# Channel-major output stages with streamed weights, and late attention spread beside them, in a hybrid encoder layer on one Trainium2 core

## The chip, the cores and the metric

One core of a Trainium2 chip runs the whole program. The metric is the device time of one execution in microseconds (us). Engines: PE = TensorE (matmul; PEld its weight loads), DVE = VectorE, ACT = ScalarE, POOL = GpSimd, SP = SyncE, which here only issues DMAs.

## The reference, cut to what matters

The sequence has 2048 tokens of 1024 channels, all in float32.

```
h    = rmsnorm(x)
proj = h @ W_in                       # 1024 -> 4096: 4 conv parts, q, k, v, az (512 each)
y_c  = c_b * causal_dwconv(c_c * c_h)            # conv group, 3 taps
z    = q @ k^T / 8                               # 8 heads of 64, strictly causal
a    = exp(log_sigmoid(z) + sum of log_sigmoid(-z) over the keys between key and query)
y_a  = a @ v
y    = group_rmsnorm([y_c, y_a]) * silu([c_z, a_z])
x    = x + y @ W_out                             # 1024 -> 1024
x    = x + sigmoid(rmsnorm(x) @ W_pg + b_pg) * (p @ W_pe)
out  = rmsnorm(x) * final_g
```

## The kernel before, in words

**Numbers and tiles.** Each float32 operand of a large product is a pair of float32r tiles, high (`hh`, `wh`) and low (`hl`, `wl`); a product is three matmuls, high by high, low by high and high by low (L208 to L210 for W_in, L543 to L545 for W_out, W_pg and W_pe). ACT writes the high part as a copy (`wh`, L200), POOL subtracts to get the low part (`wl`, L201). Tokens come in four chunks of 512 with time reversed: chunks 3 and 2 are the early half, chunks 1 and 0 the late half. A step of a projection is three matmuls on 512 columns; a projection tile (128 output channels) has 8 of them for a chunk.

**Projections.** W_in has 32 tiles of 128 channels, each run over the two chunks of a half and streamed twice, half a tile (128x512) at a time, by `load_w` and `split_half` (L187 to L202). Their results are channel-major and are evacuated by DVE.

**Attention.** For 128 queries (a row, j) and 512 keys (kc), `unit_a` (L394 to L422) issues two matmuls for z (L401, L402), two sigmoids on ACT (`s`, L405, and `b`, L407), a scan on DVE (`T`, L415; on the diagonal also L413), a copy of the last column on POOL (`carry`, L419) and the product b·T on DVE (L420). Four rows are a unit. `unit_b` (L424 to L465) then takes four key blocks: four transposes of b (L443), the high part on ACT (`ah`, L447), the low part on DVE (`al`, L448), and the two matmuls into av (L433 with `ah`, L434 with `al`). The av matmuls of a key block come directly after the transposes of the next one:

```
ah = att.tile([P, CH], F32R, tag="ah", bufs=3, ...)          # L445
...
nc.scalar.copy(ah[:, 0:w], tp[:, 0:w])                       # L447
nc.vector.tensor_tensor(out=al[:, 0:w], in0=tp[:, 0:w],
                        in1=ah[:, 0:w].bitcast(F32), op=ALU.subtract)
yield
if late:
    finish()                                                 # the av matmuls of the block before
    yield
late = (ah, al, kb, w)
```

There are 80 units: 24 in the early half (16 of them on the diagonal and so about half as large) and 56 in the late half (16 on the diagonal), head by head.

**Order of the work.** A generator, `attention`, yields after each piece; `run(rate)` pulls `rate` pieces for each projection step: `RATE_E` 0.5 in the early half, `RATE_L` 1.3 in the late half, `RATE_O` 2.0 beside the first blocks of the output stage. So the order of instructions on each engine is fixed when the program is built; the engines wait for each other by semaphores only.

**Output stages.** After the late projections W_out is loaded whole, split (`split_w`, L519 to L539; the low parts half by DVE and half by POOL) and kept on chip. `out_block` (L571) treats 16 blocks of 128 tokens, token-major (`out_prep` scales y by the group norm), and writes x1 to DRAM. W_pg and W_pe are loaded and kept likewise. The last stage (L727 to L780) reads x1 again for each block, transposes it (L742), and computes the gate, the embedding term (`pe`), the sum and the final norm; the last block is treated in quarters.

Of the kernel before, what the change touches and what calls it, by code (L numbers as in the profile page):

```python
# [9 lines left out]
BF16 = mybir.dt.bfloat16  # L10
# [5 lines left out]
P = 128  # L16
# [7 lines left out]
RATE_E = 0.5  # L24
RATE_L = 1.3
RATE_O = 2.0
LAG = 1
WARM = 9


def build(tc, xt_d, xr_d, pt_d, win_d, wout_d, wpg_d, wpe_d, cst_d, bpg_d, fg_d, out_d):
    """All token axes run backwards in time, so that attention scans forwards over keys."""
    nc = tc.nc
    ctx = ExitStack()
    with ctx:
# [7 lines left out]
        yg_d = dram.tile([SEQ // P, P, KT, P], F32, name="yg_d")  # L43
        x1_d = dram.tile([SEQ, DM], F32, name="x1_d")
        kE_d = dram.tile([NH, P, 2, CH], F32, name="kE_d")
        vE_d = dram.tile([NH, P, 2, CH], F32, name="vE_d")

# [1 line left out]
        cst = const.tile([P, 40], F32, name="cst")  # L49
# [3 lines left out]
        c_b = cst[:, 36:40]  # L53
        # first: column 0 clear, then the identity, so that row q holds a one at column q + 1
# [20 lines left out]
        rs1 = const.tile([P, 16], F32, name="rs1")  # L75
        rr = const.tile([P, 32], F32, name="rr")
# [9 lines left out]
        attx = ExitStack()  # L86
        att = attx.enter_context(tc.tile_pool(name="att", bufs=1, side="right"))
        NS = 2
# [7 lines left out]
        projx = ExitStack()  # L96
        pj = projx.enter_context(tc.tile_pool(name="pj", bufs=1, side="left"))
# [3 lines left out]
        hT, rx, rB = {}, {}, {}  # L101

        def load_x(c, kt, name, tag="w1", bufs=4):
            xt = (pj if tag == "w1" else att).tile([P, CH], F32, tag=tag, bufs=bufs, name=f"{name}{c}_{kt}")
            nc.sync.dma_start(xt, xt_d[c, kt])
            return xt

        def load_x_first(c, between=None):
            tiles = []
            for i, tag in enumerate(("q1", "q1", "q2", "q2") if c == 3 else ("kk", "kk")):  # L110
                t = att.tile([P, 2, CH], F32, tag=tag, bufs=2, name=f"xf{c}_{i}")
                for f in range(2):
                    nc.sync.dma_start(t[:, f], xt_d[c, 2 * i + f])
                    tiles.append(t[:, f])
                if i == 1 and between:
                    between()
            if c == 2:
                for i, tag in enumerate(("ke2", "ke3", "ve2", "ve3")):
                    tiles.append(load_x(c, 4 + i, "xf", tag, 1))
            return tiles  # L120

        def x_split(c, kt, xt):
            hh = pj.tile([P, CH], F32R, tag=f"hh{kt}", bufs=2, name=f"hh{c}_{kt}")
            hl = pj.tile([P, CH], F32R, tag=f"hl{kt}", bufs=2, name=f"hl{c}_{kt}")
            nc.scalar.activation(hh, xt, AF.Copy, scale=g_norm[:, kt:kt + 1])  # L125
            nc.vector.scalar_tensor_tensor(out=hl, in0=xt, scalar=g_norm[:, kt:kt + 1],  # L126
                                           in1=hh.bitcast(F32), op0=ALU.mult, op1=ALU.subtract)
            hT[c, kt] = (hh, hl)

        def norm_first(c, xts, tag):  # L130
            """r of a chunk whose x is on chip."""
            acc = None
            for kt in range(KT):
                sq = att.tile([P, CH], F32, tag="bt", bufs=10, name=f"xsq{c}_{kt}")
                if kt in (3, 5, 7):
                    nc.gpsimd.tensor_tensor(out=sq, in0=xts[kt], in1=xts[kt], op=ALU.mult)
                else:
                    nc.scalar.activation(sq, xts[kt], AF.Square)
                if kt == 0:
                    acc = sq  # L140
                else:
                    nc.vector.tensor_tensor(out=acc, in0=acc, in1=sq, op=ALU.add)
            ssp = bank(tag, 1, f"ssp{c}")
            token_sums(ssp, acc)
            norm_r(c, ssp)

        def norm_later(c):
            """r of a chunk, beside other work: a step for each tile of x."""
            acc = att.tile([P, CH], F32, tag="ke2", bufs=1, name=f"acc{c}")
            for kt in range(KT):  # L150
                xt = load_x(c, kt, "xt")
                sq = xt if kt else acc
                nc.scalar.activation(sq, xt, AF.Square)
                if kt:
                    nc.vector.tensor_tensor(out=acc, in0=acc, in1=sq, op=ALU.add)
                yield
            ssp = bank("aux", 1, f"ssp{c}")
            token_sums(ssp, acc)
            norm_r(c, ssp)

        def token_sums(ssp, sq):
            for b in range(4):
                nc.tensor.matmul(ssp[:, 2 * b:2 * b + 2], sq[:, b * P:(b + 1) * P], ones2,
                                 start=True, stop=True)

        def norm_r(c, ssp):
            r, r2 = rr[:, 8 * c:8 * c + 4], rr[:, 8 * c + 4:8 * c + 8]
            nc.vector.tensor_scalar(out=r, in0=ssp[:, 0:8:2], scalar1=1.0 / DM, scalar2=EPS,
                                    op0=ALU.mult, op1=ALU.add)
            nc.gpsimd.tensor_tensor(out=r, in0=r, in1=nhalf[:, 0:4], op=ALU.pow)  # L170
            nc.vector.scalar_tensor_tensor(out=r2, in0=r, scalar=1.0 / HD, in1=r, op0=ALU.mult,
                                           op1=ALU.mult)
            rx[c] = (r, r2)

        def norm_spread(c, tag="aux"):
            r, _ = rx[c]
            rT = bank(tag, 2 if tag == "tr" else 1, f"rT{c}")
            for b in range(4):
                nc.tensor.transpose(rT[:, b * P:(b + 1) * P], r[:, b:b + 1].to_broadcast([P, P]), ident)
            rB[c] = pj.tile([P, CH], F32, tag="rB", bufs=2, name=f"rB{c}")  # L180
            nc.scalar.copy(rB[c], rT)

# [1 line left out]
        wq, wt = [], {}  # L184

        def load_w(f):
            """Fetch and split half f of the next tile in line."""  # L187
            if not wq:
                return
            t, tag = wq[0]  # L190
            split_half(t, f, tag, pj, "wh", "wl")
            if f == 1:
                wq.pop(0)

        def split_half(t, f, tag, pool, th, tl):
            raw = pj.tile([P, CH], F32, tag="wr", bufs=2, name=f"wr{tag}_{t}_{f}")
            nc.sync.dma_start(raw, win_d[t, f])
            wh = pool.tile([P, CH], F32R, tag=th, bufs=3, name=f"wh{tag}_{t}_{f}")
# [640 lines left out]
```

## Time and profile before

| | before |
|---|---|
| time, median of 3 runs | 1733.89 us (1732.41 to 1736.25) |
| span of the profiled execution | 1731.2 us |
| busy: PE, DVE, ACT, POOL | 93%, 69%, 45%, 32% of the span |
| DMA | 152.46 MB, mean 88 GB/s |

How to read it: a span is the time from the first to the last recorded instruction of the profiled execution; the profile gives no other time of its own for that execution, and the median of the runs is 2.7 us above it. Busy times of PE overlap, since matmuls are pipelined: a 512-column matmul is shown with 0.39 to 0.50 us, while the next one starts 0.23 us after it. So 93% is not 93% of PE's peak. By place, the program is start (0 to 50 us), early half (to 525), late half with most of attention (to 1270), output stage (to 1488) and gate stage (to the end); the last av matmul of attention starts at 1311.09 us.

### The profile page before, as it was taken

To read this page: it belongs to the slowest core of one execution; us is meant where nothing else is said; L and a number is where in the kernel's file an instruction comes from. 1 tells how busy PE (TensorE), PEld (TensorE's weight loads), DVE (VectorE), ACT (ScalarE), POOL (GpSimd) and SP (SyncE) were. 2 spreads that over 40 slices of the span, in tenths; PEclk is the share of its full clock that TensorE was granted. 3 is DMA by queue.
4 is the path that set the end of the run, shared out by engine and by line. 5 is a ranking of instruction groups with operands and counts; after the bars stand their busy time and mean duration, and the time that the engine had idled before them with its cause. 6 is when DMAs were issued, how large, how long until landed. Compare 5 with 4: busy or idle time off the path is not lost.

```text
span 1731.2 us, 22033 instructions
## 1 busy us (share of the span) xinstructions
PE 1609.0 (93%) x7726; PEld 1287.3 (74%) x7726; DVE 1187.5 (69%) x1691; ACT 771.7 (45%) x1516; POOL 550.7 (32%) x607
## 2 busy tenths in 40 slices
PE   7899999999998899889898999899979999999998
PEld 5787777777877677767776777677757778788887
DVE  7676666666566898996889699978995533233333
ACT  5345345345345555564556455645563422122222
POOL 5322432432453422224223332233552111122221
PEclk9999999999999999999999999999999999999999
DMA  5413513513414311221112311221144743222221
GB/s 188 129 43 104 146 50 98 147 55 98 128 56 118 77 37 50 66 69 49 43 43 71 76 48 38 73 62 49 31 152 145 246 150 133 77 82 83 83 79 49
DMA packets 84207, 152.46 MB, mean 88 GB/s; under 512 B 9472, under 2 KB 27904, under 8 KB 84096
## 3 DMA queue, kind: packets, MB, share of 16 engines
q1 hardware_dynamic: 62304, 125.10, 24.7%
q10 hardware_dynamic: 21792, 25.96, 4.3%
q8 instruction: 61, 1.00, 0.2%
q14 instruction: 50, 0.41, 0.1%
HBM read 92.30 MB, written 33.55 MB: 73 GB/s over the span
## 4 chain that ended last, share of the span: by engine, by line
PE 55%; DVE 25%; issue 8%; ACT 5%; POOL 3%; DMA 2%; SPq 0%; ACTq 0%; DVEq 0%; POOLq 0%
DVE T L415 10%; PE pp L208 8%; PE pp L210 8%; PE pp L209 7%; DVE b L420 5%; DVE al L448 4%; PE tp L443 3%; PE pg L545 3%; PE pg L543 3%; PE pg L544 3%; PE po L543 3%; PE po L544 3%; PE po L545 3%; PE av L434 2%; ACT s L405 2%
## 5 line engine op out<-in xcount | busy, mean ns | idle before, releaser
L208 PE MATMUL pp<-hh,wh 128*128 128x512 f32 x1024 | 427.9, 418 | 0.1
L209 PE MATMUL pp<-hl,wh 128*128 128x512 f32 x1024 | 407.6, 398 | 4.4 <-DVE hl L126 4.4
L210 PE MATMUL pp<-hh,wl 128*128 128x512 f32 x1024 | 408.7, 399 | 0.0
L415 DVE TENSOR_TENSOR_SCAN T<-s,carry,small 128x513 f32<-128x513 f32 x192 | 269.7, 1411 | 28.8 <-ACT s L405 28.2
L405 ACT ACTIVATE s<-z 128x512 f32<-128x512 f32 (+1 forms) x320 | 172.2, 538 | 181.2 <-PE z L402 129.4
L201 POOL TENSOR_TENSOR wl<-wr,wh 128x512 fp32r<-128x512 f32 x128 | 184.5, 1442 | 210.4 <-ACT wh L200 152.4
L447 ACT CAST ah<-tp 128x512 fp32r<-128x512 f32 (+1 forms) x320 | 164.3, 525 | 183.1 <-PE tp L443 151.3
L420 DVE TENSOR_TENSOR b<-b,T 128x512 f32<-128x512 f32 (+1 forms) x320 | 228.0, 717 | 18.9
L210 PEld LDWEIGHTS pp<-hh,wl 128*128 128x128 f32 x1024 | 195.0, 190 | 42.3
L209 PEld LDWEIGHTS pp<-hl,wh 128*128 128x128 f32 x1024 | 196.4, 192 | 37.1 <-DVE hl L126 7.6
L448 DVE TENSOR_TENSOR al<-tp,ah 128x512 fp32r<-128x512 f32 (+1 forms) x320 | 188.3, 602 | 50.6 <-ACT ah L447 49.6
L208 PEld LDWEIGHTS pp<-hh,wh 128*128 128x128 f32 x1024 | 195.4, 191 | 29.4 <-ACT hh L125 0.7
L419 POOL COPY carry<-T 128x1 f32<-128x1 f32 x192 | 64.5, 336 | 366.7 <-DVE T L415 331.5
L443 PE MATMUL tp<-first,b 128*128 128x128 f32 x1088 | 176.6, 277 | 2.1 <-DVE b L420 1.3
L407 ACT ACTIVATE b<-z 128x512 f32<-128x512 f32 (+1 forms) x320 | 170.4, 532 | 0.0
L443 PEld LDWEIGHTS tp<-first,b 128*128 128x128 f32 x1088 | 139.1, 143 | 40.6 <-DVE b L420 5.8
L200 ACT CAST wh<-wr 128x512 fp32r<-128x512 f32 x128 | 79.4, 621 | 95.0 <-PE pp L209 73.1
L434 PE MATMUL av<-al,vv 128*128 128x512 f32 x192 | 71.9, 377 | 41.9 <-DVE al L448 41.6
L543 PE MATMUL po<-woh,yh 128*128 128x512 f32 x256 | 102.7, 402 | 2.5 <-ACT yh L567 2.5
L544 PE MATMUL po<-wol,yh 128*128 128x512 f32 x256 | 102.1, 400 | 2.2 <-DVE wol L531 2.2
L543 PE MATMUL pg<-wgh,xh 128*128 128x512 f32 (+1 forms) x272 | 102.5, 377 | 1.4 <-ACT xh L744 1.4
L545 PE MATMUL pg<-wgh,xl 128*128 128x512 f32 (+1 forms) x272 | 102.7, 378 | 0.0
(149 smaller groups left out, 2551.6 us busy)
## 6 DMA issues: line engine op xcount, KB each, us to landing
wr<-in_win_dram SPq DMA_DIRECT2D x128, 256.0 KB, 2.7
q<-sh SPq DMA_DIRECT2D x64, 128.0 KB, 2.4
q<-sl SPq DMA_DIRECT2D x64, 128.0 KB, 2.3
yg_d<-gg ACTq DMA_DIRECT2D x32, 256.0 KB, 2.3
yt<-yg_d SPq DMA_DIRECT2D x16, 512.0 KB, 3.3
xb<-in_xr_dram SPq DMA_DIRECT2D x16, 512.0 KB, 3.8
x_d<-x ACTq DMA_DIRECT2D x16, 512.0 KB, 2.6
z<-x_d SPq DMA_DIRECT2D x16, 512.0 KB, 3.3
```

The lines of the kernel that those rows point to most:

```text
L201: nc.gpsimd.tensor_tensor(out=wl, in0=raw, in1=wh.bitcast(F32), op=ALU.subtract)
L208: nc.tensor.matmul(pp, wh[:, sl], hh, start=(kt == 0), stop=False)
L209: nc.tensor.matmul(pp, wh[:, sl], hl, start=False, stop=False)
L210: nc.tensor.matmul(pp, wl[:, sl], hh, start=False, stop=(kt == KT - 1))
L405: nc.scalar.activation(s[:, 1:n + 1], zp[:, 0:n], AF.Sigmoid, scale=-0.125)
L415: nc.vector.tensor_tensor_scan(T[:, m:n + 1], s[:, m:n + 1], zeros.to_broadcast([P, n + 1 - m]), T[:, m - 1:m] if diag else carry[:, j:j + ...
L420: nc.vector.tensor_tensor(out=bt[:, 0:n], in0=bt[:, 0:n], in1=T[:, 0:n], op=ALU.mult)
L443: nc.tensor.transpose(tp[:, j * P:(j + 1) * P], bt[:, kb * P - k0:(kb + 1) * P - k0], ident)
L448: nc.vector.tensor_tensor(out=al[:, 0:w], in0=tp[:, 0:w], in1=ah[:, 0:w].bitcast(F32), op=ALU.subtract)
L543: nc.tensor.matmul(pp, ah, wh[:, sl], start=first, stop=False)
L544: nc.tensor.matmul(pp, ah, wl[:, sl], start=False, stop=False)
L545: nc.tensor.matmul(pp, al, wh[:, sl], start=False, stop=last)
```

## The change

All stages become channel-major. W_out and W_pg are appended to W_in as 16 further tiles (numbers 32 to 39 and 40 to 47) and streamed and split again for each of the four chunks, as W_in is; nothing stays resident. That doubles the weight halves split (`wh` on ACT, `wl` on POOL) from 128 to 256. The tail order is out(3), gate(3), out(2), gate(2), out(1), gate(1), out(0), gate(0).

- Late attention is ordered by chunk: all heads of chunk 1, then all heads of chunk 0. Its rows are spread over the late projections (131 rows in the order of PE), out(3) (17), gate(3) (23), out(2) (16), gate(2) (23) and out(1) (14); the early half has 96. The rates are 0.72 (early) and 0.92 (late projections and these stages).
- K, Q and V of a unit always go through DRAM (`fetch_units`, two units ahead), so SP issues 987 DMAs where it issued 520.
- z and the sigmoids of a row are issued one row earlier (`row_z` before `row_scan`; three `s` and three `T` buffers). In `second`, `al` is issued one key block after `ah`, and the av matmuls two key blocks after the transposes (four buffers of `ah` and `al`).
- b·T of odd rows goes from DVE to POOL: 160 of 320 (96 of 512 columns, 32 of 384, 32 of 128).
- The group norm and gate of y (`y_prep`, one tile of 128 channels at a time) run beside the gate stage before; the residual's square sum and the final norm work on channel-major tiles, with sums on POOL. The 128 transposes of x1 fall away. `final(c)` runs beside the next output stage; `final(0)` stands alone at the end.
- Small steps (conv taps, stores, transposes of v, norms) are put off by some steps by `later` and `tick`.

```
-RATE_E = 0.5
-RATE_L = 1.3
-RATE_O = 2.0
...
+RATE_E, RATE_L = 0.72, 0.92
...
+            eng = nc.gpsimd if j % 2 else nc.vector
+            eng.tensor_tensor(out=bt[:, 0:w], in0=bt[:, 0:w], in1=T[:, 0:w], op=ALU.mult)
...
+            for i in range(6):
+                if i < 4:
...
+                    nc.scalar.copy(ah[:, 0:nj * P], tp[:, 0:nj * P])
+                if 1 <= i <= 4:
+                    tp, ah, al, _, w = st[i - 1]
+                    nc.vector.tensor_tensor(out=al[:, 0:w], in0=tp[:, 0:w], in1=ah[:, 0:w].bitcast(F32),
+                                            op=ALU.subtract)
                 yield
...
+                if i >= 2:
+                    _, ah, al, kb, w = st.pop(i - 2)
+                    nc.tensor.matmul(av[:, 0:w], v[:, kb], ah[:, 0:w], start=diag and kb == 3, stop=False)
...
+                yt = tiles[kt][0]
+                nc.vector.tensor_tensor(out=yt, in0=yt, in1=rT, op=ALU.mult)
+                if kt >= 4:
+                    nc.gpsimd.tensor_tensor(out=yt, in0=yt, in1=tiles[kt][1], op=ALU.mult)
+                hh, _ = pair(("y", c), kt)
+                nc.scalar.copy(hh, yt)
+                if kt:
+                    low(kt - 1)
+                fetch(kt + 2)
+                rb = expand(kt + 1)
+                yield
...
+            def mix(m, e, g):
+                x1 = xs.pop(m)
+                nc.vector.tensor_tensor(out=g, in0=g, in1=e, op=ALU.mult)
+                o = resident[m] if c == 0 else g
+                nc.gpsimd.tensor_tensor(out=o, in0=x1, in1=g, op=ALU.add)
+                later(2, total, m, o)
...
+        run(workL, RATE_L)
+        for work in tail[:3]:
+            run(work, RATE_L)
```

PE's order in the late half before, at a full unit of head 0 (tp: transposes into PSUM; av: the attention output; pp: a projection; last number of al and ah: buffers, the one before it the key block, 3 first):

```order
L434 MATMUL av0_0_5377<-al0_0_1_3_5502,vv0_1_4955 128x512
L443 MATMUL tp0_0_1_1_5544<-first_69,b0_0_1_0_5297 128x128
...
L443 MATMUL tp0_0_1_1_5544<-first_69,b0_0_1_3_5405 128x128
L433 MATMUL av0_0_5377<-ah0_0_1_2_5513,vv0_1_4955 128x512
L434 MATMUL av0_0_5377<-al0_0_1_2_5514,vv0_1_4955 128x512
L443 MATMUL tp0_0_1_0_5582<-first_69,b0_0_1_0_5297 128x128
...
L443 MATMUL tp0_0_1_0_5582<-first_69,b0_0_1_3_5405 128x128
L433 MATMUL av0_0_5377<-ah0_0_1_1_5549,vv0_1_4955 128x512
L209 MATMUL pp4_1_5591<-hl1_1_4866,wh1_4_0_5370 128x512
```

Here the av matmuls of block 3 stand ahead of the transposes of block 1, and those of blocks 2 and 1 right behind the transposes of blocks 1 and 0.

And in the changed kernel at the full unit 40, also in the late projections:

```order
L504 MATMUL tp40_1_8481<-first_241,b160_8156 128x128
...
L504 MATMUL tp40_1_8481<-first_241,b163_8271 128x128
L234 MATMUL pp0_1_8445<-hh_1_3_5232,wh1_0_0_8293 128x512
L235 MATMUL pp0_1_8445<-hl_1_3_5233,wh1_0_0_8293 128x512
L236 MATMUL pp0_1_8445<-hh_1_3_5232,wl1_0_0_8294 128x512
L517 MATMUL av5_1_8283<-ah40_3_8442,vv5_1_2_7855 128x512
L518 MATMUL av5_1_8283<-al40_3_8443,vv5_1_2_7855 128x512
...
L504 MATMUL tp40_0_8517<-first_241,b160_8156 128x128
...
L517 MATMUL av5_1_8283<-ah40_2_8461,vv5_1_2_7855 128x512
L518 MATMUL av5_1_8283<-al40_2_8462,vv5_1_2_7855 128x512
```

The av matmuls of key block 3 now come behind the transposes of block 1 instead of block 2, and between transposes and av there is mostly a whole projection step, where the order before had transposes and av of neighbouring blocks side by side.

POOL's order late in the half before (carry: one column of T; wl: a low half tile of weights; sl: the low part of q and k):

```order
L419 COPY carry3_1_8435<-T3_1_1_0_8442 128x1
L201 TENSOR_TENSOR wl1_21_0_8498<-wr1_21_0_8495,wh1_21_0_8497 128x512
L419 COPY carry3_1_8435<-T3_1_1_1_8484 128x1
L419 COPY carry3_1_8435<-T3_1_1_2_8515 128x1
L419 COPY carry3_1_8435<-T3_1_1_3_8550 128x1
L419 COPY carry3_1_8435<-T3_1_2_0_8577 128x1
L238 TENSOR_TENSOR sl4_1_8590<-qk4_1_8591,sh4_1_8589 128x512
```

Four carries stand between two operations on whole tiles here.

And in the changed kernel in gate(3) (b: an odd row's product; g: the residual sum; acc: the sum of squares; wes: the low part of W_pe):

```order
L485 COPY carry3_0_11577<-T250_12169 128x1
L628 TENSOR_TENSOR acc_('o', 3)_11974<-acc_('o', 3)_11974,sq_('o', 3)_1_12112 128x512
L680 TENSOR_TENSOR wes3_3_12109<-we3_3_12062,wes3_3_12109 128x256
L226 TENSOR_TENSOR wl('x1', 3)_44_0_12207<-wr('x1', 3)_44_0_12016,wh('x1', 3)_44_0_12206 128x512
L226 TENSOR_TENSOR wl('x1', 3)_44_1_12253<-wr('x1', 3)_44_1_12104,wh('x1', 3)_44_1_12252 128x512
L485 COPY carry3_0_11577<-T251_12228 128x1
L487 TENSOR_TENSOR b251_12167<-b251_12167,T251_12228 128x512
L705 TENSOR_TENSOR g3_2_12160<-x1r3_2_11933,g3_2_12160 128x512
L680 TENSOR_TENSOR wes3_4_12215<-we3_4_12175,wes3_4_12215 128x256
```

POOL's queue, mostly copies of one column beside a split now and then, has a 512-column operation in nearly every place that isn't a copy, of five kinds.

## Rows read from the trace of the kernel before

**Rows 1.** The page's head: span, busy time and share of each engine.

```profile
span 1731.2 us, 22033 instructions
...
PE 1609.0 (93%) x7726; PEld 1287.3 (74%) x7726; DVE 1187.5 (69%) x1691; ACT 771.7 (45%) x1516; POOL 550.7 (32%) x607
```

**Rows 2.** Stretches: length; busy (x) of PE, PEld, DVE, ACT, POOL; PEclk; DMA; GB/s.

```profile
0.00:50.00 50.00, 39.01 (x150) 28.54 (x151) 35.91 (x53) 24.28 (x42) 24.22 (x25) 0.90 0.52 163
50.00:525.00 475.00, 453.32 (x2165) 364.33 (x2163) 316.51 (x493) 206.73 (x426) 173.74 (x146) 0.99 0.34 97
525.00:1270.00 745.00, 675.54 (x3323) 531.57 (x3323) 640.05 (x890) 411.31 (x822) 241.62 (x281) 0.99 0.22 60
1270.00:1488.00 218.00, 207.57 (x948) 166.82 (x949) 105.98 (x136) 68.63 (x108) 50.02 (x78) 0.98 0.47 160
1488.00:1732.00 244.00, 233.52 (x1144) 196.08 (x1142) 89.10 (x123) 60.76 (x120) 61.14 (x78) 0.99 0.21 76
```

**Rows 3.** Waits of PE from 525 to 1270 us: total, times, longest.

```profile
PE av L434 <- DVE al L448: 48.9, 59, 3.0
```

**Rows 4.** Timeline, 639 to 646 us: start, duration, instruction, [idle before <-releaser].

```profile
639.38 0.66 DVE L370 TENSOR_TENSOR u<-pp,cc 128x512 f32<-128x512 f32 x1
639.45 1.29 POOL L201 TENSOR_TENSOR wl<-wr,wh 128x512 fp32r<-128x512 f32 x1 [5.04 <-ACT wh L200]
...
639.96 1.33 DVE L420 TENSOR_TENSOR b<-b,T 128x512 f32<-128x512 f32 x1
...
641.94 0.50 PE L434 MATMUL av<-al,ve 128*128 128x512 f32 x1 [1.03 <-DVE al L448]
...
642.27 0.60 PE L443 MATMUL tp<-first,b 128*128 128x128 f32 x4
...
642.63 0.48 PE L208 MATMUL pp<-hh,wh 128*128 128x512 f32 x1
...
643.18 0.40 PE L210 MATMUL pp<-hh,wl 128*128 128x512 f32 x1
...
643.41 0.40 PE L401 MATMUL z<-kk,q 128*128 128x512 f32 x1
...
643.59 1.27 DVE L415 TENSOR_TENSOR_SCAN T<-s,carry,small 128x513 f32<-128x513 f32 x1
...
645.43 0.68 DVE L420 TENSOR_TENSOR b<-b,T 128x512 f32<-128x512 f32 x1
```

**Rows 5.** Groups by line and form: xcount | busy us, mean ns | idle before.

```profile
L415 DVE TENSOR_TENSOR_SCAN T<-s,carry,small 128x513 f32<-128x513 f32 x192 | 269.7, 1411 | 28.8 <-ACT s L405 28.2 <-POOL wl L201 0.3
...
L201 POOL TENSOR_TENSOR wl<-wr,wh 128x512 fp32r<-128x512 f32 x128 | 184.5, 1442 | 210.4 <-ACT wh L200 152.4 <-PE tp L443 30.9 <-PE z L402 25.1
L420 DVE TENSOR_TENSOR b<-b,T 128x512 f32<-128x512 f32 x224 | 184.5, 827 | 12.1
...
L377 DVE SCALAR_TENSOR_TENSOR cc<-u,cst,cc 128x512 f32<-128x512 f32 x32 | 23.8, 742 | 0.4
```

**Rows 6.** The copy of a row factor on POOL, by line and form.

```profile
L555 POOL COPY rb<-rg 128x512 f32<-128x512 f32 x16 | 9.9, 617 | 0.0
```

**Rows 7.** Timeline of a norm in the start, 23.5 to 28 us.

```profile
23.81 1.05 PE L163 MATMUL ssp<-small,xsq 128*128 128x2 f32 x8
...
25.15 1.48 POOL L170 TENSOR_TENSOR rr<-rr,small 128x4 f32<-128x4 f32 x1 [6.06 <-DVE rr L168]
...
26.68 0.65 PE L179 MATMUL rT<-first,rr 128*128 128x128 f32 x4 [1.02 <-POOL rr L170]
...
27.37 0.59 ACT L181 COPY rB<-rT 128x512 f32<-128x512 f32 x1 [5.86 <-PE rT L179]
```

**Rows 8.** Timeline of the end: the last matmul and the last DMA issue.

```profile
1722.97 0.28 PE L545 MATMUL pg<-wgh,xl 128*128 128x256 f32 x1
...
1728.27 0.34 SPq L780 DMA_DIRECT2D out_dram<-z  x1
```

**Rows 9.** DMA issues on SP: count, size of one, median us to landing.

```profile
wr<-in_win_dram SPq DMA_DIRECT2D x128, 256.0 KB, 2.7
```

More of the change, by code (lines that the diff above doesn't have):

```diff
@@ L154, in norm_later @@
                 if kt:
-                    nc.vector.tensor_tensor(out=acc, in0=acc, in1=sq, op=ALU.add)
+                    later(1, lambda xt=xt: nc.vector.tensor_tensor(out=acc, in0=acc, in1=xt, op=ALU.add))
                 yield
[L157 to L164, printed above, removed]
@@ L286, in first_proj @@
[L286 to L300 removed]
+                    nc.scalar.copy(two[i][:, :, 0:HD], vpv[:, :, i])
@@ L619, in pull, with run @@
         def pull():
-            return next(stream, False)
-        def run(rate):
-            while work:
-                need, g, after = work.pop(0)
-                while heads[0] < need:
-                    assert pull() or heads[0] >= need
-                for _ in g:
+            return next(stream, None)
+        def run(work, rate):
+            for need, make in work:
+                while any(x not in done for x in need):
+                    assert pull() is not None or all(x in done for x in need)
+                    tick()
+                for _ in make():
+                    tick()
@@ L672, in build, with add @@
[L672 to L681 removed]
+        def add(work, make, *a, need=(), tiles=()):
+            wq.extend(tiles)
+            work.append((need, lambda: make(*a)))
@@ new lines, in splits, with ahead @@
+        def splits(c):
+            for kt in range(KT):
+                xt = load(xt_d[c, kt], f"xu{c}_{kt}")
+                yield
+                x_split(c, kt, xt)
+                if kt == KT - 1:
+                    norm_spread(c, "tr", 2)
+        def ahead(g, n):
+            alive = True
+            while alive:
+                for _ in range(n):
+                    if next(g, "end") == "end":
+                        alive = False
+                yield
+        conv = [[("c", i), ("h", i), ("b", i), ("g", i)] for i in range(4)]
@@ new lines, in build @@
+        wq.extend([(24, cE[0]), (16, cE[0])])
+        workE = pairs_of(cE, orderE, last=ahead(splits(1), 2))
+        workL = pairs_of(cL, orderL, last=y_prep(3), first_besides=ahead(splits(0), 2))
+        fetch_w()
+        x3 = []
+        for i in range(8):
+            tag, n = (("kk", 4), ("q1", 2), ("q2", 2))[0 if i < 4 else 1 if i < 6 else 2]
+            t = att.tile([P, CH], F32, tag=tag, bufs=n, name=f"xf3_{i}")
+            nc.sync.dma_start(t, xt_d[3, i])
+            x3.append(t)
@@ L693, in build @@
         norm_spread(2, "av")
-        first_proj(cE, True)
-        run(RATE_E)
-        work.extend(later)
-        run(RATE_L)
-        projx.close()
-        order = list(range(8, 16)) + list(range(0, 8))
-        outx = ExitStack()
-        po = outx.enter_context(tc.tile_pool(name="po", bufs=1, side="left", reuse_waits="tile"))
-        wout = split_w(po, wout_d, KT, "wo", raw_bufs=4)
-        blocks = [(b, order[i + 1] if i % 8 < 7 else None) for i, b in enumerate(order)]
-        for b, after in blocks[:3]:
-            add(0, out_block(b, after))
```

1030 lines of the change are left out of this document (530 added, 500 removed).

## Prediction

> **What bounds the kernel now.** I read the page's head first: PE is busy 93% of 1731.2 us, and no other engine above 69% [rows 1]. Busy matmuls overlap, so I priced PE by spacing: a 512-column matmul lets the next begin .23 us later (643.18 to 643.41), a group of four transposes .36 us later (642.27 to 642.63) [rows 4]. The products are 4800 such matmuls in both kernels (1600 steps of three): 1104 us. A full attention unit has 16 of them and four groups of transposes, 16 x .23 + 4 x .36 = 5.1 us, one on the diagonal by its widths about 3.2: 48 x 5.1 + 32 x 3.2 = 347. With some 60 us of small operations PE needs about 1515 us. Everything above that, some 215 us, is what a change of order can win.
>
> The table of stretches says where they lie [rows 2]. Summing each stretch's matmuls by those spacings: start, 27 of 50; early half, 435 of 475; late half and output stage, 813 of 963; gate stage, 234 of 243. So 150 of the loss lies where late attention is. There DVE is the crowded engine: 640.05 of 745 us busy, against 105.98 of 218 and 89.10 of 244 in the two stages behind. The work of attention stops at 1311 us while DVE idles half of the rest.
>
> What PE waits for there is one thing: av for `al`, 48.9 us in 59 waits [rows 3]. The timeline shows one: POOL's `wl` runs 639.45 to 640.74; DVE's b, begun at 639.96, ends only at 641.29, .55 us after it, and takes 1.33 instead of the .68 that it has at 645.43; `al` stands behind it on DVE, and av begins 1.03 us late, at 641.94, released by `al` [rows 4]. So DVE and POOL hold each other up: means are 827 ns for b and 1411 for a scan that takes 1.27 alone [rows 4, 5].
>
> **The change part by part.** The sum is against the span; the median of the runs is 2.7 us above it.
>
> *Start:* the same chain, 50 us.
>
> *Deeper pipeline.* `al` gets one more piece of work ahead of its reader, av two; between transposes and av lies a step of three matmuls (.69 us) or more. The waits of about .8 us (48.9 / 59) mostly go; the longest of 3.0 us do not. What is late next is DVE itself wherever it has more work than PE.
>
> *Spreading.* By the order of PE, 131 attention rows remain in the late projections, and 93 go beside out(3), gate(3), out(2), gate(2), out(1). The contents, PE by spacing and DVE by rows 4 and 5 (scan 1.27, b .68, evacuations .66, `al` taken like b, scaled forms .74), are then: early PE 438, DVE 289; late projections 516 and 384; out(3) 67 and 50, gate(3) 86 and 73, out(2) 66 and 54, gate(2) 86 and 74, out(1) 70 and 57; gate(1), out(0), gate(0), without attention, 57, 47, 57 on PE. In no stretch is DVE's own work above PE's; before, it was close to PE's in the late half.
>
> *POOL.* It gains 128 halves of `wl`, 160 products b·T, the residual sums and the square sums: 551 us becomes about 950. As an engine it has room, but it shares with DVE. From the pair in rows 4, b had done about .13 of its .68 when it was held (it ended .55 after POOL), so an operation of 1.29 can hold DVE for 1.29 - .13 = 1.15. Lower bound of the cost: nothing, if the two never meet or DVE's next operation reads PSUM and isn't held. Upper bound: each POOL operation holds DVE in full. For gate(3) that is 44 operations of 512 columns (16 `wl`, 9 b, 8 sums, 7 square sums, 4 of `y_prep`) x 1.15 = 51, and 7 for small ones: 58 on top of 73, 131 us. Between: DVE operations that read PSUM (`al`, evacuations, half of its 73) go on while POOL works, and only the other half, 37, excludes it: 37 + 58 = 95. I take this, since the evacuation u, which reads PSUM and began .07 us ahead of the same `wl`, took .66 us beside it [rows 4]. The same sum gives 62, 66, 96 and 64 for out(3), out(2), gate(2), out(1), 372 for the late projections.
>
> *Stage times.* In the early half before, PE got 435 of 475, or .92, with one-deep pipelining and 67% of DVE busy. I divide the larger of PE's content and the shared 37 + 58 kind of sum by .92: out(3) 73, gate(3) 102, out(2) 73, gate(2) 102, out(1) 78 (its end drains attention): 428. Early and late projections keep a smaller loss, because the waits for `al` go: 438 + 25 = 463 and 516 + 34 = 550. The three stages without attention I take at the gate stage's 234 / 243 = .96: 60 + 49 + 60 = 169.
>
> The Trainium skill, page "Perfetto Trace Analysis", section "Optimizing Scalar/DVE Operations", says that GPSIMD and DVE share an SBUF read port, so that offloading between those two might not help. By that rule the move of 160 products is worth nothing and the new splits cost DVE time; read strictly it gives the slow rival below. The trace agrees that they collide, by the b that ended .55 us after POOL's `wl`.
>
> *`y_prep`.* Per attention tile a chain: row factors on POOL .62 [rows 6], transposes .36, DVE .68, POOL 1.29, about 2.95 us, between steps of PE of 1.2 to 1.6 us. Waits of some 1.5 us for 4 tiles of 4 chunks bound it at 24; other attention work fills some of that: 16. Nothing is the lower bound.
>
> *Weights and DMAs.* K, Q, V and weights by DRAM: SP's issues go from 520 to 987. A half tile lands 2.7 us after issue [rows 9]; weights are fetched three halves (over 15 us) ahead, units two ahead (10 us), so I cost them at nothing. If SP stood waiting for a Q buffer with weights queued behind it, this would show up as PE waiting for `wh`.
>
> *Tail.* Before, the last matmul started at 1722.97 and the span ended 8 us later [rows 8]. Now a chain: evacuation .66, sigmoid .6, product .68, POOL sum 1.29, square .6, POOL sum 1.29, token sums 1.05, power 1.48, transposes .65, copy .59, eight scalings of .74, and the last store about 2.7: 17 us [rows 4, 5, 7, 9].
>
> *Sum:* 50 + 463 + 550 + 428 + 169 + 16 + 17 = 1693 us of span, and with 2.7 a time of **1696 us**.
>
> **The rivals.**
>
> *PE-bound.* Deep pipelining hides all collisions: the five mixed stretches run at PE / .95 = 375 / .95 = 395, late projections 530, early half 455, `y_prep` nothing: 50 + 455 + 530 + 395 + 169 + 17 = 1616, with 2.7 a time of 1619. For it: PE's wait was one kind only [rows 3]. Against: DVE's mean scan is stretched already with POOL at 32% [rows 1, 5].
>
> *The pipeline moves no time.* The waits of PE only move from av to the next instruction that needs DVE (z for a buffer of s), because the throughput of DVE and ACT with latencies set the pace; with the same loss as before, about 1734. Against it: DVE is idle half of the last 460 us.
>
> *Slow: the collisions serialise.* One mechanism: in the five mixed stretches almost every DVE operation meets a POOL one and waits it out. The holds then add to DVE's work: out(3) 85, gate(3) 131, out(2) 90, gate(2) 132, out(1) 92, 530 instead of 428: 1798. It turns slower than before once over 38 of these 102 us come true, that is if a mean scan in gate(3) exceeds about 1.75 us. Half of it gives 1747. For it: b's mean is 827 ns against .68 alone while POOL was a third busy, and in gate(3) POOL's queue is full. Against it: the evacuation u passed unheld [rows 4]. By the Trainium skill's rule on the shared port it is the case to expect where two queues are both full.
>
> **How the numbers follow.** Forecast .48, with its own range from 1660 to 1728 (sharing sums and `y_prep` at 0 or 24, the loss per stage from .90 to .95); PE-bound .20; no gain .07; slow .25. 0.2% is about what a measurement of this kernel can tell from no change: below 1730.4 is faster, above 1737.4 slower. So faster .68 (forecast and PE-bound), same .07, slower .25. For 8 in 10 the range runs from 1612, which takes in most of the PE-bound case, to 1772, which takes the weaker half of the slow one and leaves its upper end out.
>
> **What would show it.** Right: PE's wait of av for `al` under 20 us in the whole trace; mean scan near 1500 ns; POOL about 950 us busy, DVE 1080 to 1130; gate(3) and gate(2) about 100 us long with DVE about 90% busy; the last matmul some 17 us before the end. Wrong: a late half projection stretch over 580 us or a scan above 1.75 us (slow rival), gate(3) under 92 us (PE-bound), PE waiting for `wh` or for K and V (my zero for the DMAs), a long PE idle at `gT` or at the first product of an output stage (`y_prep` mis-sized).

## The result, and the profile after

The changed kernel takes 1746.09 us (median of 4 runs, 1743.46 to 1750.3) against 1734.11 (4 runs) before: a ratio of 1.0073, with a 95% interval from 1.0056 to 1.0091. It is slower by .7%, where 1696 and faster were forecast. The profiled execution's span is 1745.9 us.

The page's head of the changed kernel:

```profile
span 1745.9 us, 23060 instructions
...
PE 1614.3 (92%) x7634; PEld 1309.7 (75%) x7634; DVE 1217.3 (70%) x1544; ACT 855.6 (49%) x1680; POOL 966.2 (55%) x891
```

Against [rows 1], POOL has risen from 550.7 to 966.2 us, as forecast. DVE has 147 instructions fewer and is busy 30 us longer: what was moved off it came back as longer operations.

The table of stretches of the changed kernel, cut at its own stages (each begins with the first matmul of its first step): early half, late projections, then out(3), gate(3), out(2), gate(2), out(1), gate(1), out(0), and gate(0) with the tail (columns as in [rows 2]):

```profile
50.00:519.60 469.60, 452.09 (x2186) 370.70 (x2185) 314.95 (x462) 209.49 (x440) 210.96 (x189) 0.98 0.44 132
519.60:1056.60 537.00, 529.00 (x2605) 434.64 (x2604) 408.95 (x523) 271.81 (x540) 251.42 (x263) 0.99 0.41 123
...
1056.60:1146.30 89.70, 76.86 (x347) 61.70 (x346) 72.27 (x78) 46.40 (x89) 71.14 (x60) 0.90 0.50 156
1146.30:1257.80 111.50, 98.68 (x457) 78.34 (x456) 88.41 (x95) 65.23 (x129) 83.28 (x79) 0.92 0.49 151
1257.80:1340.40 82.60, 71.76 (x330) 57.96 (x330) 67.91 (x75) 45.88 (x89) 49.26 (x47) 0.94 0.59 188
1340.40:1452.00 111.60, 95.00 (x454) 75.27 (x453) 84.20 (x91) 63.27 (x123) 80.87 (x74) 0.95 0.47 144
1452.00:1531.00 79.00, 71.55 (x347) 56.93 (x345) 70.74 (x78) 46.12 (x89) 58.21 (x48) 0.98 0.57 180
1531.00:1612.70 81.70, 68.65 (x299) 54.71 (x298) 28.53 (x38) 34.18 (x61) 54.74 (x47) 0.90 0.50 154
1612.70:1663.50 50.80, 47.84 (x205) 38.09 (x204) 23.86 (x26) 20.28 (x34) 32.30 (x25) 0.97 0.69 228
1663.50:1746.00 82.50, 62.55 (x265) 50.43 (x263) 21.45 (x29) 28.82 (x51) 49.89 (x41) 0.86 0.34 109
```

Up to 1056 us the change did what was forecast: 1056.6 us for start, early half and late projections, forecast 1063 (the early half 469.6 against 463, the late projections 537.0 against 550). In the late projections DVE is busy 76% (408.95 of 537.00), where the late half before had 86% [rows 2]. All of the miss lies behind. The five mixed stages take 474.4 us instead of 428, the rest 215.0 instead of 202 (169 + 16 + 17). gate(1) misses most, by 22 us before its share of `y_prep`; the last of attention falls into its first 10 us (the last av matmul starts at 1540.86 us), where the prediction had it in out(1); out(3) misses by 17, gate(3), out(2) and gate(2) by 10 each, out(1) by 1.

What PE waited for in the whole trace after (columns as in [rows 3]):

```profile
PE tp L504 <- DVE al L512: 25.0, 15, 3.2
PE pe L722 <- ACT wes L679: 12.0, 3, 7.6
PE gT L604 <- DVE yt L606: 10.1, 7, 3.7
PE vp L297 <- DVE vT L291: 6.8, 5, 2.6
PE rT L171 <- POOL rr L161: 6.5, 10, 1.4
PE ssp L156 <- POOL acc_('o', 0)_16764 L628: 5.7, 1, 5.7
PE gT L604 <- POOL rb L590: 5.6, 2, 4.8
PE ssp L156 <- POOL acc_('o', 3)_11974 L628: 5.0, 1, 5.0
```

The wait of av for `al` (48.9 us in [rows 3]) is nearly gone (1.8). A smaller one came for it: transposes that wait until `al` has freed their bank. New are waits at the seams between stages: for the split weights of W_pe (`wes`), for `y_prep` (gT), and for POOL's square sums (the ssp rows, one for each norm). I also added up, behind 1040 us, every space of PE that is more than .35 us longer than the columns of its matmul need at .23 us for 512: some 63 us stand at seams ahead of the last norm, and 27 at attention and evacuations.

DVE's operations in the mixed stages (1056.6 to 1531 us), by line and form as in [rows 5], below the stretch itself:

```profile
1056.60:1531.00 474.40, 413.84 (x1926) 330.20 (x1924) 383.53 (x414) 266.90 (x516) 342.75 (x305) 0.94 0.52 162
```

```profile
L481 DVE TENSOR_TENSOR_SCAN T<-s,carry,small 128x513 f32<-128x513 f32 x72 | 115.9, 1610 | 26.3 <-ACT s L462 25.6 <-POOL wl('x1', 3)_44_0_12207 L226 0.5
L512 DVE TENSOR_TENSOR al<-tp,ah 128x512 fp32r<-128x512 f32 x79 | 52.6, 675 | 6.3 <-ACT ah L509 6.2
L487 DVE TENSOR_TENSOR b<-b,T 128x512 f32<-128x512 f32 x41 | 47.0, 1145 | 2.5
```

A scan takes 1610 ns (1411 in [rows 5], 1.27 us alone), b 1145 (.68 alone); `al`, which reads PSUM, takes 675 and isn't stretched. The prediction counted DVE's own work there at 50 + 73 + 54 + 74 + 57 = 308 us; it is busy 383.5, so by that count POOL held it for 75 us. The slow rival's full sum was 222 (530 - 308). Its mechanism was at work at a third of its strength, and its point of decision for gate(3), a mean scan above 1.75 us, was not reached (1569 there). So holding, as that rival sums it, doesn't explain the loss.

### The profile page after: what moved, and what is told of

It is laid out like the page before. It is cut to its first block, busy times and chain, and to the rows that moved or that the text cites. A ratio compares the mean times of both kernels' runs of the same rounds, so it can differ in the third digit from the quotient of the medians.

```text
span 1745.9 us, 23060 instructions
## 1 busy us (share of the span) xinstructions
PE 1614.3 (92%) x7634; PEld 1309.7 (75%) x7634; DVE 1217.3 (70%) x1544; ACT 855.6 (49%) x1680; POOL 966.2 (55%) x891
## 5 line engine op out<-in xcount | busy, mean ns | idle before, releaser
L236 PE MATMUL pp<-hh,wl 128*128 128x512 f32 x1008 | 401.8, 399 | 0.0
L481 DVE TENSOR_TENSOR_SCAN T<-s,carry,small 128x513 f32<-128x513 f32 x192 | 293.5, 1529 | 98.0 <-ACT s L462 94.2
L487 POOL TENSOR_TENSOR b<-b,T 128x512 f32<-128x512 f32 (+2 forms) x160 | 179.7, 1123 | 150.2 <-DVE T L481 110.5
L226 POOL TENSOR_TENSOR wl<-wr,wh 128x512 fp32r<-128x512 f32 x126 | 176.3, 1401 | 101.3 <-ACT wh L225 95.3
L485 POOL COPY carry<-T 128x1 f32<-128x1 f32 x192 | 53.4, 278 | 277.6 <-DVE T L481 236.6
L487 DVE TENSOR_TENSOR b<-b,T 128x512 f32<-128x512 f32 (+1 forms) x160 | 149.1, 932 | 10.4 <-DVE T L481 0.5
L479 DVE TENSOR_TENSOR_SCAN T<-s,first 128x129 f32<-128x129 f32 x128 | 84.0, 658 | 61.8 <-ACT s L462 58.1
L459 PE MATMUL z<-kk,q 128*128 128x512 f32 (+1 forms) x320 | 118.7, 371 | 5.9 <-DMA kk<-qk_d 3.9
L518 PE MATMUL av<-al,vv 128*128 128x512 f32 (+1 forms) x320 | 120.1, 376 | 1.8 <-DVE al L512 1.8
L517 PE MATMUL av<-ah,vv 128*128 128x512 f32 (+1 forms) x320 | 119.3, 373 | 0.0
L460 PE MATMUL z<-kk,q 128*128 128x512 f32 (+1 forms) x320 | 119.1, 372 | 0.0
```

The lines of the kernel that those rows point to most:

```text
L226: nc.gpsimd.tensor_tensor(out=wl, in0=raw, in1=wh.bitcast(F32), op=ALU.subtract)
L236: nc.tensor.matmul(pp, wl[:, sl], hh, start=False, stop=(kt == KT - 1))
L481: nc.vector.tensor_tensor_scan(T[:, m:w + 1], s[:, m:w + 1], zeros.to_broadcast([P, w + 1 - m]), T[:, m - 1:m] if diag else carries[h, qc] ...
L487: eng.tensor_tensor(out=bt[:, 0:w], in0=bt[:, 0:w], in1=T[:, 0:w], op=ALU.mult)
L518: nc.tensor.matmul(av[:, 0:w], v[:, kb], al[:, 0:w], start=False, stop=kc == 3 and kb == 0)
```

## Experiments

Names: A, shared port; B, seams; R, ring of buffers; D, depth; S and M, density of attention; P and Q, POOL's load or not. "Before" is timed in every comparison again, at 1732.4 to 1734.4.

**e1_bt_dve**, the offload undone:

```
-            eng = nc.gpsimd if j % 2 else nc.vector
+            eng = nc.vector
```

> The changed kernel with every product b*T on DVE again; POOL loses 160 operations (about 180 us busy), DVE gains them. Theory A (shared port): the holds of POOL on DVE cost the mixed stages their time; the mean 513-column scan falls from 1529 ns to under 1450, and the time falls by 15 us or more, to 1731 or less. Theory B (seams: PE stands at the heads of chains where one stage gives way to the next, 63 us in 40 waits behind norm sums, weights of the embedding and y_prep): the seams stay, time within 10 us of 1746. Theory C (offloading helps, DVE is the bound of the mixed stages): slower than 1756.

1741.29 us, 1.0049 of before (1.0031 to 1.0067). POOL's busy time falls by 167 us, DVE's rises by only 46, to 1263.2, though 160 products come back to it; a scan falls to 1491 ns. At 96 x .68 us and less for the narrower ones they are some 90 us of work, so the offload spared DVE only half of what it took off. The time differs by 5 us, at the edge of what the two intervals tell apart. C falls and A's sizes were not reached; B's band holds.

**e2_norms**, **e3_wes**, **e4_yprep**: one seam each.

```
-            later(2, spread)
+            later(5, spread)
...
+            for _ in range(8 if c else 0):
+                yield
             norm_r(8 + c, accs["o", c])
```

> The token sums of a norm are issued later on PE: three more steps behind an output stage, eight more steps into the next output stage for the final norm. Theory B: the waits of PE for POOL's square sums and for the power, 24.5 us ahead of the last norm, go, and some 5 us of half-rate matmuls behind them: 1716 to 1724. Theory A: PE's waits only move to the next instruction that needs DVE or POOL: 1738 or more.

1739.79 us, 1.0032 (1.0012 to 1.0052): 6 us, where B had 22 and more. Half of the edit had no effect: a gate stage flushes all deferred steps at its head (`tick_all`), so the sums of x1 stood where they had been, and only those of the final norm moved.

```
+                if m == 6:
+                    p_prep(c)
+                    pe_weights(c, 0)
                 yield from stage(OUT0 + m, ("y", c), evac(m), besides)
```

> The embedding inputs and the first weights of W_pe are fetched and split two tiles before the end of the output stage, not at the head of the gate stage. Theory B: PE's waits for wes (13.3 us in three long waits and their followers) go and 2 to 4 us of half-rate matmuls: 1728 to 1734. Theory A: no change, 1742 or more.

1750.59 us, 1.0091 (1.0055 to 1.0126), not distinguishable from the changed kernel; the waits for `wes` are still 12.2. They stand in the middle of the gate stages, not at their heads. The timeline of the changed kernel in gate(1) shows the largest:

```profile
1567.08 0.33 SPq L674 DMA_DIRECT2D we<-in_wpe_dram  x1
...
1569.18 0.41 ACT L679 CAST wes<-we 128x256 fp32r<-128x256 f32 x1 [0.26 <-DMA we<-in_wpe_dram]
1569.63 0.79 PE L722 MATMUL pe<-ph,wes 128*128 128x512 f32 x1 [7.55 <-ACT wes L679]
```

PE stands 7.55 us for weights whose load SP issued only 2.5 us earlier. In SP's queue ahead of it are the loads of `y_prep` and of x1, which take their buffers from the same ring of five (`w1`).

For e4_yprep, `spaced(g, 6)` puts six steps of the gate stage behind each piece of `y_prep`:

```
-                return gate_stage(c, y_prep(c - 1) if c else None)
+                return gate_stage(c, spaced(y_prep(c - 1), 6) if c else None)
```

> y_prep of chunks 2, 1 and 0 advances by one tile every seven steps of the gate stage before, not every step; the one beside the last late projection stays. Theory B: 11 us of PE's waits at gT go, with 2 us of half-rate: 1732 to 1738. Theory A: the same operations spread out hold DVE as long in sum, no change, 1742 or more.

1756.21 us, 1.0133 (1.0114 to 1.0152): slower by 10, which neither theory had. I took it that slower steps hold the ring's buffers longer, and this suggested R.

**e5_ring**, **e8_ring_yp**, **e9_seams**, each on top of the one before:

```
-                    xs[m] = load(x1_d[c][m], f"x1r{c}_{m}")
+                    xs[m] = load(x1_d[c][m], f"x1r{c}_{m}", "xr")
```

> The x1 tiles that a gate stage reads again get two buffers of their own and are fetched in their own tile's turn; they leave the ring of five buffers that the weights of W_pe, the tiles of y_prep and they shared (paid for by three instead of four buffers of split weights). Theory R (SP stands in front of a load whose ring buffer is still held, and the loads of W_pe and of y behind it come late): the waits of PE for wes, 12.0 us with one of 7.6, fall below 3 us, and the time to 1728 to 1738. Theory T (the mixed stages run at what DVE and POOL can do, and a wait taken away comes back as another): 1742 or more.

1743.25 us, 1.0057 (1.0042 to 1.0072). The waits for `wes` fall from 12.0 us to 1.8, so R names their cause; but 3 us come of it, which the intervals hardly tell from nothing. The rest came back as other waits: all of PE's spaces over .35 us behind 50 us, added up as above, fell only by 3, from some 127 us to some 124.

> The same, and y_prep of chunks 2, 1 and 0 advances every third step of the gate stage, not every step, which without the buffers made it slower by 10 us. Theory R: now the waits at gT beside gate stages, 11 us, go too: 1715 to 1728. Theory T: 1740 or more.

1739.82 us, 1.0035 (1.0023 to 1.0048): neither R's size nor far from T's. The slower `y_prep` doesn't hurt here, but gains 3 us, not 15. It is slowed less than in e4_yprep (`spaced(..., 2)`, not 6), and no run has this spacing without the buffers, so it stays open whether the ring was what hurt there.

For e9_seams the added lines of e2_norms (the eight steps) and of e3_wes come with these:

```
-            later(2, spread)
+            later(4, spread)
...
-                p_prep(c)
-                pe_weights(c, 0)
-                tick_all()
                 return gate_stage(c, spaced(y_prep(c - 1), 2) if c else None)
```

> The same, and the norms' token sums come later: four steps into the gate stage (nothing flushes them at its head now) and eight steps later in the final norm; the first weights of W_pe are split in the output stage. Theory R (with the seams): another 20 us of waits for square sums and powers go: 1695 to 1712. Theory T: 1735 or more.

1721.03 us, .992 (.9905 to .9935): now faster than before, by 19 us more, between the two theories. gate(1) takes 71.5 us instead of 81.7 in the changed kernel, gate(3) 105 instead of 111.5.

**e14_norms_only** took only this last edit, without ring and spacing:

> The changed kernel with only the later token sums and the earlier split of W_pe of e9_seams, without its x1 buffers and slower y_prep. If the 19 us between e8_ring_yp and e9_seams belong to the norms: 1724 to 1731. If they need the other two edits, so that the loads come in time: 1738 or more.

1740.02 us, 1.003 (1.0017 to 1.0043): 6 us alone, 19 with the others. The seams are not a sum of waits: one that is taken away is worth its length only when the load or the sum behind it is in time too.

**e6_one**, the depth undone:

```
-                if 1 <= i <= 4:
-                    tp, ah, al, _, w = st[i - 1]
+                if i < 4:
+                    tp, ah, al, _, w = st[i]
...
-                if i >= 2:
-                    _, ah, al, kb, w = st.pop(i - 2)
+                if i >= 1:
+                    _, ah, al, kb, w = st.pop(i - 1)
```

> The changed kernel with the depth of before: al follows ah at once, the av matmuls come one key block behind the transposes. Theory D (the depth is what took PE's waits for al out of the late projections, where its loss fell from about 120 us to about 25): 1775 or more, PE's waits of av for al back above 30 us. Theory S (the thinner spread of attention did it, since DVE is less crowded): within 10 us of 1746, waits for al below 30 us.

1754.38 us, 1.0118 (1.0103 to 1.0133): 8 us slower than the changed kernel. Its early half and late projections, and its wait of av in the whole trace:

```profile
50.00:515.90 465.90, 449.75 (x2186) 367.29 (x2185) 307.15 (x463) 210.58 (x440) 213.80 (x189) 0.99 0.44 134
515.90:1074.80 558.90, 544.97 (x2691) 445.24 (x2689) 432.21 (x553) 291.97 (x573) 269.25 (x279) 0.99 0.40 121
```

```profile
PE av L518 <- DVE al L512: 13.0, 15, 2.8
```

Without the depth, out(3) starts 18 us later (at 1074.8 us, not 1056.6): the early half is 4 us shorter, the late projections 22 longer. Part of the 22 is work and not loss: a unit has fewer pieces with one-deep pipelining, so more of attention falls into the late projections (PE has 2691 matmuls there, not 2605) and it ends earlier; 10 us come back later. D is far too large, and S's bands hold: even one-deep, PE's av waits only 13 us for `al`, not 48.9.

**e7_rate**, **e11_seams_r115**: more attention beside the late projections.

```
-        run(workL, RATE_L)
+        run(workL, 1.3)
```

> The changed kernel with 1.3 pieces of attention for each late projection step instead of .92: 179 rows beside the late projections instead of 131, 45 beside out(3), gate(3) and out(2), none beside gate(2) and out(1). Theory S (the thinner spread is what freed the late projections): DVE is again too full there and PE waits more than the later stages save: 1752 or more. Theory M (a row costs less beside projections, where the changed kernel loses 22 us in 560, than beside output and gate stages, where it loses 100 in 474): 1738 or less.

1803.93 us, 1.0396 (1.0368 to 1.0425). M falls at once. But S's reason does not hold either; the late projections and PE's waits in them:

```profile
518.80:1198.90 680.10, 620.68 (x2985) 501.58 (x2983) 520.00 (x654) 345.76 (x688) 309.68 (x324) 0.96 0.36 110
```

```profile
PE z L459 <- DMA kk<-qk_d: 18.0, 8, 4.0
PE gs L363 <- ACT sq L356: 16.8, 5, 4.2
```

DVE is busy 76% there, as in the changed kernel. Attention runs up against the projections: it asks for K as soon as it has been written to DRAM, and PE stands for the load. How much thinner attention is worth by itself stays open.

> e9_seams with 1.15 pieces for each late projection step: 163 rows beside the late projections instead of 131, and no attention left beside out(1). Theory M: 1705 to 1716. Theory S: 1724 or more.

1742.85 us, 1.0054 (1.0036 to 1.0072), 22 us slower than e9_seams: the same, weaker (waits for K 6.5 us).

**e10_seams_bt**, **e12_seams_sums**: all b·T on DVE in the mended kernel, then the sums of the last chunk too.

> e9_seams (own x1 buffers, y_prep every third step, norms later, W_pe earlier) with all products b*T on DVE. If the offload costs by itself (POOL's share of b*T made the changed kernel 5 us slower): 1713 to 1718. If its cost was only that POOL's sums came late at the seams, which are mended: 1719 to 1724. If DVE is now the bound: over 1726.

1722.39 us, .992 (.9894 to .9945): the same as e9_seams within the intervals. That fits an offload whose 5 us were lateness at the seams, but the bands are no wider than the spread of the runs (1719.96 to 1725.06), so it isn't shown.

```
+            eng = nc.gpsimd if key[1] else nc.vector
+            eng.tensor_tensor(out=accs[key], in0=accs[key], in1=sq, op=ALU.add)
...
-                nc.gpsimd.tensor_tensor(out=o, in0=x1, in1=g, op=ALU.add)
+                (nc.gpsimd if c else nc.vector).tensor_tensor(out=o, in0=x1, in1=g, op=ALU.add)
```

> e10_seams_bt with the residual sum and the square sums of chunk 0 on DVE, not POOL; no attention runs there, and DVE is under a third busy. The waits of PE for the last square sums (3.0 and 5.7 us) and the tail behind the last product shorten, by 1.29 - .68 = .6 us for each of three operations in the tail's chain and by the queue ahead of them: 4 to 8 us faster than e10_seams_bt if POOL's queue holds the chain there, within 2 us of it if not.

1716.04 us, .9883 (.9858 to .9909): 6 us, as expected.

**e13_nosplit**: the streamed splits.

```
+                if t < OUT0:
+                    nc.gpsimd.tensor_tensor(out=wl, in0=raw, in1=wh.bitcast(F32), op=ALU.subtract)
+                wt[t, tag, f] = (wh, wl if t < OUT0 else wh)
```

> The changed kernel without POOL's subtraction for the low weight parts of the 16 output and gate tiles: their third matmul uses the high part again, so the low parts are left out of the result; matmuls, DMAs and ACT's copies stay. POOL loses 128 operations, about 175 us, nearly all from 1050 us on. Theory P (POOL's full queue in the mixed and last stages is what costs there, by holding DVE and by late sums): the stretch from out(3) to the end, 689 us, shortens by 25 us or more: 1721 or less. Theory Q (the stages' chains and order cost, not POOL's load): 1736 or more.

1698.02 us, .9792 (.977 to .9815): 48 us less than the changed kernel with nothing else altered. Its mixed stages, and the scan and b there:

```profile
1054.70:1491.00 436.30, 400.27 (x1925) 323.94 (x1924) 332.51 (x414) 265.69 (x516) 214.89 (x224) 0.96 0.56 176
```

```profile
L483 DVE TENSOR_TENSOR_SCAN T<-s,carry,small 128x513 f32<-128x513 f32 x72 | 107.8, 1497 | 34.7 <-ACT s L464 34.1 <-POOL b L489 0.3
...
L489 DVE TENSOR_TENSOR b<-b,T 128x512 f32<-128x512 f32 x41 | 33.7, 821 | 3.3 <-ACT b L466 0.9
```

The mixed stages lose 38 us (474.4 to 436.3), DVE 51 us of busy time for about 80 splits, .64 us each. P's number holds. Of its two reasons only the first shows, DVE held: in the mixed stages PE's waits add up to 60 us in the changed kernel and 36 here, and of the 24 that go, 20 are waits that a DVE operation ended (34 to 14) and 2 are waits that POOL ended (19 to 17). The largest is that of the transposes for `al`, ahead of which the held scan and b stand in DVE's queue; in the changed kernel and here:

```profile
PE tp L504 <- DVE al L512: 15.3, 11, 3.0
```

```profile
PE tp L506 <- DVE al L514: 1.4, 3, 0.6
```

The other 14 us are gaps too short to be listed and the clock (last section): the matmul spacings at its lower level fall from 146 to 93. Without the subtraction the buffers of these weights also come free earlier, but that can't be the price: in the changed kernel PE's waits for the weights of W_out and W_pg add up to .3 us.

The seams' waits, for W_pe and for the sums, are nearly all still there.

**e15_wl_dve**, **e16_wl_dve_bt**: the splits kept, but on DVE, on top of e12_seams_sums.

```
-                nc.gpsimd.tensor_tensor(out=wl, in0=raw, in1=wh.bitcast(F32), op=ALU.subtract)
+                (nc.gpsimd if t < OUT0 else nc.vector).tensor_tensor(out=wl, in0=raw, in1=wh.bitcast(F32),
+                                                                     op=ALU.subtract)
```

> e12_seams_sums with the 128 subtractions of the output and gate tiles on DVE, not POOL. From e13_nosplit a split on POOL holds DVE by about .64 us in the mixed stages ((383.5 - 332.5) / 80), and on DVE it would take about .68 by itself. If that hold is the whole price: DVE as full as before, POOL's sums earlier, 1708 to 1718. If DVE's own queue is worse than the hold, since PE waits for the split behind attention's work: 1722 or more. If POOL's lateness was most of the price: under 1705.

1695.84 us, .9783 (.977 to .9796): the best version of the study, 50 us below the changed kernel and 2.2% faster than before. The mixed stages, their scan, and the wait of the transposes for `al` there, in e12_seams_sums:

```profile
1057.90:1516.00 458.10, 403.02 (x1926) 323.71 (x1924) 393.20 (x462) 267.30 (x516) 286.25 (x257) 0.96 0.54 169
```

```profile
L481 DVE TENSOR_TENSOR_SCAN T<-s,carry,small 128x513 f32<-128x513 f32 x72 | 116.2, 1614 | 19.0 <-ACT s L462 18.4 <-issue 0.3
```

```profile
PE tp L504 <- DVE al L512: 22.3, 12, 5.1
```

And in e15_wl_dve:

```profile
1054.60:1497.40 442.80, 399.43 (x1925) 320.18 (x1925) 400.24 (x544) 266.66 (x516) 172.02 (x176) 0.97 0.55 174
```

```profile
L482 DVE TENSOR_TENSOR_SCAN T<-s,carry,small 128x513 f32<-128x513 f32 x72 | 105.9, 1470 | 12.7 <-ACT s L463 12.6
```

```profile
PE tp L505 <- DVE al L513: 14.1, 13, 2.2
```

In e15_wl_dve DVE takes 80 more operations in the mixed stages (54 us at .68) and is busy only 7 us longer, because as many holds go. So the hold was about as dear as the operation itself. Of the 20 us between the two kernels, 15 lie in the mixed stages. They aren't lateness of POOL's own results: PE's waits there that POOL ended stay (6 us and 7), and those that DVE ended fall from 47 to 31. With the same sum of busy time, DVE is held less at the scan and at b (908 to 742 ns), which end in `al` and so in PE's wait, and works on a split, for which PE doesn't wait, instead. This is read from the traces; no run holds DVE at other operations alone.

> e15_wl_dve with the odd rows' b*T on POOL, so that DVE gives 160 products of attention for 128 splits. If a POOL operation costs DVE about what its own would: within 4 us of e15_wl_dve. If DVE is the bound of the mixed stages: 6 us or more faster than it.

1701.3 us, .9812 (.9793 to .983): 5.5 us slower than e15_wl_dve, just outside the first band. Even with POOL half empty, giving it b·T gains nothing; here a result of POOL itself is late, the row factors of `y_prep`, for which PE waits 10.6 us instead of 5.5. DVE is the fuller engine in e15_wl_dve (77%), yet it wins, so DVE's throughput is not the bound.

## Why the prediction was wrong

**Right.** The place of the old loss; the end of av's waits for `al`; start, early half and late projections together (1056.6 against 1063); POOL's busy time (966 against 950); that an operation of DVE with an operand in PSUM goes on beside POOL (`al` with 675 ns in the mixed stages, .68 us in [rows 4] for an unheld b).

**Wrong by size: the sum 37 + 58, the sharing of DVE and POOL.** The term for the mixed stages was 428 us, and 474.4 were measured. By that working the 16 splits of a stage (16 x 1.15 = 18 us) cost nothing in the output stages, where PE's content was the larger, and without them gate(3) and gate(2) would fall to PE's content, 86 / .92 = 93 instead of 102: 18 us in all. Measured: 38 in the mixed stages, 48 in the kernel. The step treated two resources that are each less than full as if the larger sum alone set the time. DVE was not that full: 79% and 75% in gate(3) and gate(2), where about 90% was expected, though its busy time in the whole kernel was 1217 us and not 1080 to 1130. PE follows chains through DVE in a fixed order, and pays when the operation that is held stands in front of its own: with out(3) at 67 us of PE content and 62 of shared sum it took 89.7. The other part of the miss there isn't the splits': without them 436.3 us are left, where the same working gives 410.

**Wrong by omission: norms and loads at the seams.** `y_prep` had a term (16), the sums ahead of a norm, the second half of a chain of POOL additions, had none; nor had W_pe's loads, whose cover ("three halves") is true of the big weights only. The sentence that SP's issues cost nothing failed by the mechanism that it named itself, a held buffer with a load queued behind it, at another buffer. PE's idle time at `gT`, the prediction's sign of a mis-sized `y_prep`, appeared as well: 15.7 us, 4.8 the longest. Mending these seams was worth 25 us (1746.1 to 1721.0), in e9_seams.

**The rivals.** The slow rival came closest in time (1747 at half strength), partly for its reason: holds of 75 us of the 222 that it had in full, and the price of the splits came through DVE. Its sum still misses the mechanism, as e15_wl_dve shows, where the holds are replaced by as much work of DVE and the time falls by 20: which operations were held counted, and not DVE's total. That its half strength meets the measured time is luck, since 25 us of the miss belong to seams that it doesn't have. The Trainium skill, page "Perfetto Trace Analysis", section "Optimizing Scalar/DVE Operations", says that offloading operations between GPSIMD and DVE might not help. These runs agree: the move of b·T to POOL cost 5.5 us in e16_wl_dve_bt and about 5, at the edge of the noise, in e1_bt_dve, and e10_seams_bt shows no difference.

**Lucky.** I put the freed late projections down to the deeper pipeline. Without it they are 22 us longer, part of which is work moved there, and the kernel 8 us (e6_one). The rest of the fall from the loss before, some 120 us from 525 to 1270, goes with thinner attention, which no run isolates: e7_rate shows only that more of it runs into its own inputs. And most of that loss only moved: by the prediction's own contents of PE, the mixed stages lose 474.4 - 375 = 99 us.

## What to carry to other kernels

When streamed weights replace resident ones, count the splits as work of the engine that makes them, and ask which operations of another engine they hold up: 128 subtractions on POOL cost 48 us here, and with the seams mended 20 us came back when DVE made them, at no fewer operations. At the head of an in-order PE queue put nothing that ends a chain through other queues (a norm's sums, a fresh weight): let it stand some steps later, and give each stream of loads its own buffers. Mend such waits together and time them together: one at a time they gained 6 us, nothing clear of the noise, and lost 10; together and with buffers of their own they gained 25.

## What the runs showed of the hardware

After a long idle time PE ran slower for a while, which no term had. The timeline at the head of out(2) in the changed kernel:

```profile
1261.08 0.39 PE L235 MATMUL pp_('y', 2)_12836<-hl_('y', 2)_4_11872,wh('y', 2)_32_1_12725 128*128 128x512 f32 x1
...
1266.51 1.87 PE L156 MATMUL ssp<-small,acc_('o', 3)_11974 128*128 128x2 f32 x8 [5.05 <-POOL acc_('o', 3)_11974 L628]
...
1271.07 0.63 PE L235 MATMUL pp_('y', 2)_12836<-hl_('y', 2)_5_11894,wh('y', 2)_32_1_12725 128*128 128x512 f32 x1
1271.50 0.63 PE L236 MATMUL pp_('y', 2)_12836<-hh_('y', 2)_5_11893,wl('y', 2)_32_1_12726 128*128 128x512 f32 x1
1271.92 0.63 PE L459 MATMUL z<-kk,q 128*128 128x512 f32 x1
```

Behind a wait of 5.05 us, matmuls of 512 columns start .43 us apart, not .23: the lower of the two clock levels, 1.2 GHz. The granted clock (PEclk, the third column from the end) shows the same: half from 1266.3 to 1273.1 us, full before and after.

```profile
1256.10:1266.30 10.20, 5.36 (x25) 4.12 (x24) 8.80 (x9) 4.87 (x10) 7.10 (x7) 1.00 0.20 55
1266.30:1273.10 6.80, 6.19 (x21) 5.43 (x22) 1.76 (x4) 0.61 (x2) 2.40 (x3) 0.50 0.30 111
1273.10:1280.00 6.90, 6.90 (x37) 5.62 (x37) 6.65 (x8) 5.95 (x11) 2.69 (x3) 1.00 0.68 227
```

The changed kernel's trace has 146 such spacings of .38 to .5 us and that of before 85: (146 - 85) x .2 = 12 us, with mean granted clocks of .961 and .986. So this wait cost more than its length; and in the table of stretches the granted clock is .86 to .98 from out(3) on, where [rows 2] had .98 and .99 in the last two stages.
